# State space stage of a two-block transformer: transposes of x and y behind later products, half of the output additions on ScalarE and GpSimd

## The chip, the cores and the metric

The kernel runs on one core of a Trainium2 chip. The core has five engines with a queue of instructions each: TensorE (PE, matrix products and transposes), VectorE (DVE), ScalarE (ACT), GpSimd (POOL) and SyncE (SP, which issues DMAs). Each queue is worked off in order; semaphores make one engine wait for another. The metric is the time of one execution on the device in microseconds, the median over runs.

## The reference, cut to what matters

The program is two transformer blocks on 1024 tokens of width 1024, in float32. The change lies in the first layer of the second block. Its state space part and its convolution part share one input product and one output product:

```python
def even_layer(x, ...):
    proj = rmsnorm(x, norm_w) @ w_in
    z_a, xbc, dt_raw, glu_v, glu_g, z_b = jnp.split(proj, idx, axis=-1)
    xs, bs, cs = split(silu(causal_dwconv(xbc, conv_w, conv_b)))     # 4 taps
    y = ssd_chunked(xs, dt, a, bs, cs, d_skip) * silu(z_a)
    y_a = rmsnorm(y by group, ssd_norm_w)                            # 4 groups of 256
    u = causal_dwconv(glu_v * sigmoid(glu_g), dw_w, dw_b)            # 31 taps
    y_b = silu(layernorm(u, ln_w, ln_b)) * silu(z_b)
    return x + concatenate([y_a, y_b]) @ w_out

# ssd_chunked, for each chunk of 128 tokens and each head
y_diag = (cm @ bm.T * exp(segment sums)) @ (x * dt)
y_off  = exp(cs) * (cm @ state);   state = state * exp(cs[-1]) + bm.T @ (x * dt * decay)
y      = y_diag + y_off + x * d_skip
```

## The kernel before

Products of a weight with an activation are made from float32 numbers split in a high and a low part, three matmuls for one (L263 to L265, in `mm3`). ScalarE casts the high part of a weight (L197), VectorE and GpSimd subtract it from the weight for the low part (L202). PSUM gives four buffers of 512 columns (`pa`) and two of 1024 (`pb`), handed out in the order in which the program asks for them; a buffer is free for the next product when its last reader is done.

`even` makes the state space part in four groups g of four heads, and puts two of eight channel tiles of the convolution part into each group:

- z for eight token tiles (product, tanh on ScalarE, L1376 on VectorE), then a gated unit `glu`: two products in `pb`, a tanh, VectorE's L1331, and `conv31`, thirty VectorE steps (L1311) whose place in the queue is put back by 500 places, and which end in GpSimd's sum over channels, usum (L1312).
- `xbc` makes B, C and two tiles of x: product, three VectorE steps (L1351), a tanh on ScalarE (L1353) and a last step on VectorE (L1354). `x_tr(j, ...)` transposes a tile of x, tokens to partitions, in eight transposes on TensorE (L1408), with two copies on ScalarE (L1409).
- For each half i of the tokens (512): the product of B and C (L1453, copied by ScalarE at L1455), and for each of the four heads a segment product with its mask (L1459, L1460), the exponential on ScalarE (L1464) and the product with B C on GpSimd (L1465). This gives the matrices MT.
- For each half and each of its four token tiles m: y from MT x (L1484) and C state (L1485), VectorE (L1487, L1488), GpSimd (L1489, adds x d_skip) and VectorE (L1490, times silu z); and the new state (L1496, L1499).
- At the end of a half the four tiles of y are transposed back (L1505, eight transposes), scaled on ScalarE (L1508) and written to DRAM (L1509).
- Products of gate halves, z_b (`gate_half`: ScalarE L1341, VectorE L1342, which frees the PSUM buffer), are spread between these steps.

The order in which an engine takes its instructions is set by a planner that follows the order in which the code is written (its priority), put back or forward where `later` says so, and lets a ready instruction pass one that it expects to wait.

`conf` makes the output. `ya_load(g)` loads y of a group, casts it (ScalarE L1527) and subtracts (VectorE L1528); `out_proj` then makes for each of eight token tiles t and two halves hf of the columns six matmuls, and adds the result, times rstd, to h on VectorE (`add_h`, L292). Called y0 to y3 for the four groups. Between them stand the LayerNorm of the convolution part: the mean, u minus mu on VectorE (L1550), squares on ScalarE (L1555), their sum over eight channel tiles on GpSimd (L1556), and then u times rb (L1578, of each pair one on VectorE and one on GpSimd), which begins the four parts cp of the convolution part's output (L1580 to L1586, with additions at L290). In `out_proj` there is another way for half of the additions, `spread`, used by other stages of the kernel: ScalarE scales into a tile `tmp` (L305) and GpSimd adds it to h (L306).

## Time and profile before

| | us |
|---|---|
| median of three runs | 3098.76 (3096.89 to 3098.79) |
| the profiled execution | 3093.24 |
| its span, first to last instruction | 3091.2 |
| TensorE busy | 2907.2 |
| VectorE busy | 2062.9 |
| ScalarE busy | 1196.4 |
| GpSimd busy | 1014.5 |

The state space stage lies at about 1480 to 2190 us of the span, the output stage behind it until 2390. The rows below come from the page of the profile (busy times), from the view of who waited for whom, from the view of stretches of time with the granted clock of TensorE, from the groups by line, and from the timeline, in which an instruction's idle time before it stands in brackets with what ended it. Durations in the timeline are in us, those by line in ns.

### The profile page before, as it was taken

The numbers are of one execution on the slowest core, as the hardware profiler recorded it, in microseconds if no ns is written. First come the engines' busy times: TensorE is split into PE (matmuls) and PEld (weight loads), VectorE is DVE, ScalarE is ACT, GpSimd is POOL, SyncE is SP. The second block draws the span as 40 slices with busy tenths as digits, with TensorE's granted clock in tenths as the row PEclk, the third lists the DMA queues.
The fourth block names the chain that finished last, engine by engine and source line by source line (L and its number), as shares of the span: only waits on it lengthen the run. The fifth ranks groups of instructions, "written<-read, shape, count | busy, mean of one in ns | idle before, by whom it ended". The sixth has DMA issues, their size and how long they took to land.

```text
span 3091.2 us, 39184 instructions
## 1 busy us (share of the span) xinstructions
PE 2907.2 (94%) x14470; PEld 2364.7 (76%) x14470; DVE 2062.9 (67%) x3296; ACT 1196.4 (39%) x2264; POOL 1014.5 (33%) x917
## 2 busy tenths in 40 slices
PE   8999899898799999999998989999999999999998
PEld 7777676677588887788877878787777888878776
DVE  4225889865755555443798979787698454178786
ACT  5421666634433333221432322323234332155654
POOL 2112610122555554321125151524331231121444
PEclk9999999899899999999999999999999999999999
DMA  3012100212122223421311211122522446244531
GB/s 120 28 48 66 35 1 8 69 42 75 48 82 82 85 86 117 166 96 44 99 48 55 62 48 48 59 59 68 211 75 96 121 143 186 78 139 143 167 93 65
DMA packets 179380, 259.93 MB, mean 84 GB/s; under 512 B 16606, under 2 KB 107254, under 8 KB 179190
## 3 DMA queue, kind: packets, MB, share of 16 engines
q1 hardware_dynamic: 157813, 219.69, 22.4%
q10 hardware_dynamic: 16768, 20.98, 2.1%
q0 software_dynamic: 4608, 16.78, 1.4%
q8 instruction: 114, 1.87, 0.2%
q14 instruction: 77, 0.62, 0.1%
HBM read 191.33 MB, written 66.06 MB: 83 GB/s over the span
## 4 chain that ended last, share of the span: by engine, by line
PE 66%; DVE 15%; issue 5%; POOL 4%; ACT 3%; DMA 3%; SPq 0%; POOLq 0%; ACTq 0%; DVEq 0%
PE pa_t L263 16%; PE pa_t L264 16%; PE pa_t L265 15%; PE pb_t L265 3%; PE pb_t L264 3%; PE pb_t L263 3%; DVE acc_t L1311 3%; PE pa_t L941 2%; PE pb_t L1036 1%; PE pa_t L1055 1%; DVE wl_t L202 1%; PE pb_t L1750 1%; PE pb_t L1751 1%; ACT wh_t L197 1%; DVE h_t L292 1%
## 5 line engine op out<-in xcount | busy, mean ns | idle before, releaser
L202 POOL TENSOR_TENSOR wl_t<-wr_t,wh_t 128x349 fp32r<-128x349 f32 (+3 forms) x199 | 239.0, 1207 | 976.0 <-ACT wh_t L197 942.2
L263 PE MATMUL pa_t<-wh_t,x_t 128*128 128x512 f32 (+3 forms) x1024 | 374.3, 366 | 2.6 <-DVE xl_t L212 0.8
L264 PE MATMUL pa_t<-wl_t,x_t 128*128 128x512 f32 (+3 forms) x1024 | 371.3, 363 | 0.3 <-DVE wl_t L202 0.3
L1311 DVE SCALAR_TENSOR_TENSOR acc_t<-u_t,c,acc_t 128x1024 f32<-128x1024 f32 x240 | 339.4, 1416 | 2.9
L197 ACT CAST wh_t<-wr_t 128x1024 fp32r<-128x1024 f32 (+2 forms) x199 | 175.5, 890 | 354.2 <-PE pb_t L264 138.3
L290 DVE TENSOR_TENSOR h_t<-h_t,pa_t 128x512 f32<-128x512 f32 x256 | 173.1, 684 | 175.3 <-PE pa_t L265 171.8
L202 DVE TENSOR_TENSOR wl_t<-wr_t,wh_t 128x675 fp32r<-128x675 f32 (+2 forms) x173 | 170.9, 991 | 169.1 <-ACT wh_t L197 168.6
L263 PE MATMUL pb_t<-x_t,wh_t 128*128 128x512 f32 x608 | 244.3, 402 | 3.7 <-ACT wh_t L197 2.9
L265 PE MATMUL pb_t<-x_t,wl_t 128*128 128x512 f32 x608 | 242.2, 399 | 1.0 <-DVE wl_t L202 1.0
L264 PE MATMUL pb_t<-x_t,wh_t 128*128 128x512 f32 x576 | 231.0, 401 | 0.0
L265 PE MATMUL pa_t<-wh_t,x_t 128*128 128x512 f32 (+3 forms) x640 | 221.4, 346 | 0.0
L263 PEld LDWEIGHTS pa_t<-wh_t,x_t 128*128 128x128 f32 x1024 | 192.3, 188 | 33.6 <-ACT wh_t L197 1.8
L264 PEld LDWEIGHTS pa_t<-wl_t,x_t 128*128 128x128 f32 x1024 | 192.5, 188 | 30.9 <-DVE wl_t L202 2.0
L265 PE MATMUL pa_t<-wh_t,xl_t 128*128 128x512 f32 x512 | 200.4, 392 | 3.0 <-POOL xl_t L1848 2.1
L326 ACT CAST wh_t<-wr_t 128x512 fp32r<-128x512 f32 x154 | 92.1, 620 | 243.0 <-POOL wr_t L334 129.3
L263 PE MATMUL pa_t<-x_t,wh_t 128*128 128x512 f32 x400 | 163.9, 410 | 2.8 <-ACT xt_t L382 2.1
L265 PE MATMUL pa_t<-x_t,wl_t 128*128 128x512 f32 x400 | 158.8, 397 | 0.0
L327 DVE TENSOR_TENSOR wl_t<-wr_t,wh_t 128x512 fp32r<-128x512 f32 x110 | 97.7, 907 | 91.0 <-ACT wh_t L326 91.0
L263 PE MATMUL pa_t<-xh_t,wh_t 128*128 128x512 f32 x352 | 138.9, 395 | 5.3 <-DVE tmp_t L454 4.8
L263 PEld LDWEIGHTS pb_t<-x_t,wh_t 128*128 128x128 f32 x608 | 115.5, 190 | 30.8 <-ACT wh_t L197 3.9
L264 PE MATMUL pa_t<-xt_t,wh_t 128*128 128x512 f32 x352 | 138.2, 392 | 0.4 <-DVE xt_t L366 0.4
L265 PE MATMUL pa_t<-xh_t,wl_t 128*128 128x512 f32 x352 | 137.8, 392 | 0.0
(558 smaller groups left out, 7477.9 us busy)
## 6 DMA issues: line engine op xcount, KB each, us to landing
wr_t<-in_a_w_in SPq DMA_DIRECT2D x46, 512.0 KB
wr_t<-in_c_w_in SPq DMA_DIRECT2D x26, 512.0 KB
wr_t<-in_ffn_w_gate SPq DMA_DIRECT2D x22, 512.0 KB
wr_t<-in_ffn_w_up SPq DMA_DIRECT2D x22, 512.0 KB
yf<-o_t SPq DMA_DIRECT2D x22, 512.0 KB
wr_t<-in_ffn_w_down SPq DMA_DIRECT2D x44, 256.0 KB
yr_t<-yf SPq DMA_DIRECT2D x22, 512.0 KB
h_t<-in_x SPq DMA_DIRECT2D x16, 512.0 KB
```

The costliest lines, as they stand in the source:

```text
L197: nc.scalar.copy(hi, raw)
L202: e.tensor_tensor(*[x[:, c] for x in f], op=ALU.subtract)
L263: mm(out, lh, rh, start=st, stop=False)
L264: mm(out, lh, rl, start=False, stop=False)
L265: mm(out, ll, rh, start=False, stop=en)
L290: self.nc.vector.tensor_tensor(h[t][:, c], h[t][:, c], ps, op=ALU.add)
L292: self.nc.vector.scalar_tensor_tensor(h[t][:, c], ps, rstd[:, t:t + 1], h[t][:, c], op0=ALU.mult, op1=ALU.add)
L326: nc.scalar.copy(hi, src)
L327: eng.tensor_tensor(lo, src, hi.bitcast(F32), op=ALU.subtract)
L941: self.nc.tensor.transpose(pt[:, i * 256 + q * P:i * 256 + (q + 1) * P], w[t0 + q][:, (b0 + i) * P:(b0 + i + 1) * P], self.ident)
L1036: mm(sp[:, c0:c0 + wd], qT[:96, hd, t * P:(t + 1) * P], kT[:96, hd, c0:c0 + wd], start=True, stop=c0 + wd < n)
L1311: nc.vector.scalar_tensor_tensor(acc, u[:, k:k + S], cw31(k, c), acc, op0=ALU.mult, op1=ALU.add)
```

## The change

Three things. `x_tr(1, x1)`, the transposes of the group's second tile of x, moves from between the MT matrices of half 0 and those of half 1 to behind both. The transposes of y become a function `y_tr`, called later: for half 0 behind the first products (MT x and C state) of half 1, for half 1 behind the next group's first z product, and at once only at the very end. In `conf` the four y parts call `out_proj` with `spread=1`: in each token tile the second half's addition is made by ScalarE (L305) and GpSimd (L306), and the first half's stays on VectorE. The pool of `conf` gets two tmp tiles for it.

```diff
--- before.py
+++ after.py
@@ -1355,6 +1355,18 @@
             return o
 
         st8 = lambda tag: self.sb.tile([P, NT, 16], F32, name=tag, tag=tag, bufs=1)
+        turn_y = []
+
+
+        def y_tr(g, i, ys):
+            for j in range(2):
+                ps = self.psum()
+                for m in range(4):
+                    tr(ps[:, m * P:(m + 1) * P], ys[m][:, j * P:(j + 1) * P], self.ident)
+                yt = self.slot("zb", [P, 512])
+                nc.scalar.activation(yt, ps, AF.Copy, scale=gss[:, 2 * g + j:2 * g + j + 1])
+                nc.scalar.dma_start(out=ysp[2 * g + j, :, i * 512:i * 512 + 512], in_=yt)
+
         glu_w(0)
         for g in range(4):
             segs = [(g * 256, 256)] + ([(3072, 16)] if g == 0 else [])
@@ -1366,6 +1378,8 @@
             if g == 0:
                 dtr = st8("dtr")
             for t in range(NT):
+                if t == 1 and turn_y:
+                    y_tr(*turn_y.pop())
                 ps = self.psum()
                 nw = 272 if g == 0 else 256
                 tk = slice(t * P, (t + 1) * P)
@@ -1465,8 +1479,7 @@
                     nc.gpsimd.tensor_tensor(M, M, cb, op=ALU.mult)
                     MT[i, e] = M
                 spread()
-                if i == 0:
-                    x_tr(1, x1)
+            x_tr(1, x1)
             if g < 3:
                 glu(2 * g + 2)
             for i in range(2):
@@ -1483,6 +1496,8 @@
                     for e in range(4):
                         mm(ps[:, e * 64:(e + 1) * 64], MT[i, e][:, m * P:(m + 1) * P], xd[:, e * 64:(e + 1) * 64])
                     mm(ps[:, 256:512], cT[:, tk], state)
+                    if turn_y:
+                        y_tr(*turn_y.pop())
                     y = self.small(256, tag="y", bufs=4)
                     nc.vector.tensor_tensor(b4(y), b4(ps[:, 256:512]), self.bc(ecs[:, t, hs], 64), op=ALU.mult)
                     nc.vector.tensor_tensor(y, y, ps[:, 0:256], op=ALU.add)
@@ -1499,14 +1514,9 @@
                         nc.vector.tensor_tensor(ns, ns, ps[:, :256], op=ALU.add)
                         state = ns
                     spread()
-                for j in range(2):
-                    ps = self.psum()
-                    for m in range(4):
-                        tr(ps[:, m * P:(m + 1) * P], ys[m][:, j * P:(j + 1) * P], self.ident)
-                    c = slice(i * 512, i * 512 + 512)
-                    yt = self.slot("zb", [P, 512])
-                    nc.scalar.activation(yt, ps, AF.Copy, scale=gss[:, 2 * g + j:2 * g + j + 1])
-                    nc.scalar.dma_start(out=ysp[2 * g + j, :, c], in_=yt)
+                turn_y.append((g, i, ys))
+                if (g, i) == (3, 1):
+                    y_tr(*turn_y.pop())
             self.rsqrt(rstd, ss, 256 * 4, EPS, 8)
 
     def conf(self, hs, usum, rs, spill, zsp, ysp):
@@ -1527,7 +1537,7 @@
                 nc.scalar.copy(yh, y)
                 nc.vector.tensor_tensor(yl, y, yh.bitcast(F32), op=ALU.subtract)
                 ys.append((yh, yl))
-            return lambda ts=range(NT): self.out_proj(h, ys, w, rstd=rs[g], ts=ts)
+            return lambda ts=range(NT): self.out_proj(h, ys, w, rstd=rs[g], ts=ts, spread=1)
 
         y0 = ya_load(0)
         h = self.load_h(hs)
@@ -1994,7 +2004,7 @@
                     with K.pool("even", bc=2, u=2, sz=2, xs=2, bk=1, zb=2, MT=6, cb=1, tmp=2):
                         K.even(X, usum, rs, spill, zsp, ysp)
                 hctx = K.open(K.pool("h2", "right", h=8))
-                with K.pool("conf", u8=8, z=2, c=6, y2=8):
+                with K.pool("conf", u8=8, z=2, c=6, y2=8, tmp=2):
                     h, st = K.conf(hs, usum, rs, spill, zsp, ysp)
         if "E" in stages:
             h3 = dt("h3", [S, D])
```

Lines behind the change move: in `even` by 14 or 15 (L1408 becomes L1422, L1453 L1467, L1459 L1473), the transposes of y become L1365, and in `conf` lines move by 10 (L1556 becomes L1566, L1578 L1588).

TensorE, group 1, at the transposes of the second tile of x (`g_t`) before: `pb_t` products are those of the gated unit, `bc_t` those of B and C, `csT` the segment products.

```order
L263 MATMUL pb_t<-x_t,wh_t 128x512
L1408 MATMUL pa_t<-c_72,g_t 128x128 x8
L1453 MATMUL pa_t<-bc_t 128x128 x4
L1459 MATMUL pa_t<-csT,c_97 128x512
L1460 LDWEIGHTS c_99
L1460 MATMUL pa_t<-c_92,c_99 128x512
```

The same place after (the row here begins at the third of the segment products):

```order
L1473 MATMUL pa_t<-csT,c_97 128x512
L1474 LDWEIGHTS c_99
L1474 MATMUL pa_t<-c_92,c_99 128x512
L264 MATMUL pb_t<-x_t,wh_t 128x512
L1473 MATMUL pa_t<-csT,c_97 128x512
L1474 LDWEIGHTS c_99
L1474 MATMUL pa_t<-c_92,c_99 128x512
L1422 MATMUL pa_t<-c_72,g_t 128x128 x4
L265 MATMUL pb_t<-x_t,wl_t 128x512
L1422 MATMUL pa_t<-c_72,g_t 128x128 x4
L263 MATMUL pb_t<-x_t,wh_t 128x512
L264 MATMUL pb_t<-x_t,wh_t 128x512
```

The transposes of x stood first; they now stand behind the product of B and C, all four segment products and one product of the gated unit, and are cut in two.

TensorE, group 1, end of half 0, before: eight transposes of y stand ahead of half 1's first products (`xd_t,MT_t`, then `sst,bc_t`).

```order
L265 MATMUL pa_t<-x_t,wl_t 128x512
L1505 MATMUL pa_t<-c_72,y_t 128x128 x8
L1484 MATMUL pa_t<-xd_t,MT_t 128x64 x4
L1485 MATMUL pa_t<-sst,bc_t 128x256
L263 MATMUL pb_t<-x_t,wh_t 128x512
L1496 MATMUL pa_t<-xd_t,bk_t 128x256
L264 MATMUL pb_t<-x_t,wh_t 128x512
L265 MATMUL pb_t<-x_t,wl_t 128x512
L1484 MATMUL pa_t<-xd_t,MT_t 128x64 x4
```

After:

```order
L265 MATMUL pa_t<-x_t,wl_t 128x512
L1497 MATMUL pa_t<-xd_t,MT_t 128x64 x4
L1498 MATMUL pa_t<-sst,bc_t 128x256
L1365 MATMUL pa_t<-c_72,y_t 128x128 x8
L263 MATMUL pb_t<-x_t,wh_t 128x512
L264 MATMUL pb_t<-x_t,wh_t 128x512
L1511 MATMUL pa_t<-xd_t,bk_t 128x256
L265 MATMUL pb_t<-x_t,wl_t 128x512
L1497 MATMUL pa_t<-xd_t,MT_t 128x64 x4
```

The transposes of y have changed places with the first products of half 1; the next such product, which takes the second tile m, stands as far behind as before.

GpSimd, output stage, y0 to y2, before: usum additions L1556 (seven) between low parts of weights.

```order
L1489 TENSOR_TENSOR y_t<-y_t,xs_t 128x256
L202 TENSOR_TENSOR wl_t<-wr_t,wh_t 128x349
L1489 TENSOR_TENSOR y_t<-y_t,xs_t 128x256
L202 TENSOR_TENSOR wl_t<-wr_t,wh_t 128x349 x2
L1556 TENSOR_TENSOR usum_t<-usum_t,c_t 128x1024 x4
L202 TENSOR_TENSOR wl_t<-wr_t,wh_t 128x349
L1556 TENSOR_TENSOR usum_t<-usum_t,c_t 128x1024 x3
L202 TENSOR_TENSOR wl_t<-wr_t,wh_t 128x349 x3
```

After (L1566 is the usum addition, L306 the additions to h):

```order
L202 TENSOR_TENSOR wl_t<-wr_t,wh_t 128x349
L306 TENSOR_TENSOR h_t<-h_t,tmp_t 128x512 x4
L1566 TENSOR_TENSOR usum_t<-usum_t,c_t 128x1024 x2
L306 TENSOR_TENSOR h_t<-h_t,tmp_t 128x512
L1566 TENSOR_TENSOR usum_t<-usum_t,c_t 128x1024
L306 TENSOR_TENSOR h_t<-h_t,tmp_t 128x512
L1566 TENSOR_TENSOR usum_t<-usum_t,c_t 128x1024
L306 TENSOR_TENSOR h_t<-h_t,tmp_t 128x512
L1566 TENSOR_TENSOR usum_t<-usum_t,c_t 128x1024 x3
L306 TENSOR_TENSOR h_t<-h_t,tmp_t 128x512
L202 TENSOR_TENSOR wl_t<-wr_t,wh_t 128x349 x2
L306 TENSOR_TENSOR h_t<-h_t,tmp_t 128x512 x7
```

The seven usum additions now stand between the additions to h: two ahead of tile 4 of y1, the other five between tiles 4 and 7.

## Rows read from the trace of the kernel before

**Rows 1.** From the page, part 1: busy us (share of the span) xinstructions of each engine

```profile
PE 2907.2 (94%) x14470; PEld 2364.7 (76%) x14470; DVE 2062.9 (67%) x3296; ACT 1196.4 (39%) x2264; POOL 1014.5 (33%) x917
```

**Rows 2.** Busy time by engine in the output stage's first half (us, then busy (xinstructions) by engine)

```profile
2195.00:2300.00 105.00, 93.81 (x414) 73.96 (x412) 89.70 (x105) 33.97 (x34) 45.74 (x19) 1.00 0.41 152
```

**Rows 3.** Who TensorE waited for, 1480 to 2200 us: us in total, times, longest

```profile
PE pa_t L1408 <- DVE g_t L1354: 12.5, 5, 3.3
...
PE pa_t L1505 <- DVE y_t L1490: 7.4, 11, 1.3
```

**Rows 4.** The same for 2200 to 2330, 2230 to 2260 and 2285 to 2293 us

```profile
PE pa_t L263 <- DVE h_t L292: 8.8, 7, 1.6
...
PE pa_t L263 <- DVE h_t L292: 3.8, 3, 1.6
...
PE pa_t L263 <- DVE h_t L292: 2.0, 2, 1.2
```

**Rows 5.** Timeline of TensorE, group 1: start us, us, instruction [idle before <-releaser]

```profile
1785.63 1.06 PE L1408 MATMUL pa_t<-c,g_t 128*128 128x128 f32 x8 [3.09 <-DVE g_t L1354]
...
1791.13 0.39 PE L265 MATMUL pb_t<-x_t,wl_t 128*128 128x512 f32 x1
...
1791.36 0.40 PE L263 MATMUL pb_t<-x_t,wh_t 128*128 128x512 f32 x1
```

**Rows 6.** Timeline of VectorE and ScalarE, same place

```profile
1784.26 1.22 DVE L1354 SCALAR_TENSOR_TENSOR g_t<-g_t 128x1024 f32<-128x1024 f32 x1
...
1786.60 0.68 DVE L1342 SCALAR_TENSOR_TENSOR zb_t<-zb_t,pa_t 128x512 f32<-128x512 f32 x1
...
1784.13 0.58 ACT L1341 ACTIVATE zb_t<-pa_t 128x512 f32<-128x512 f32 x1
```

**Rows 7.** Windows behind the x waits of groups 0 and 1; PEclk after POOL is the granted clock

```profile
1624.50:1628.20 3.70, 3.42 (x24) 2.53 (x24) 3.70 (x6) 2.45 (x7) 1.67 (x2) 1.00 0.54 175
...
1785.50:1790.70 5.20, 5.07 (x24) 3.49 (x25) 5.17 (x6) 3.38 (x10) 1.77 (x3) 0.67 0.13 50
```

**Rows 8.** Timeline of VectorE at group 1's gated unit; GpSimd and TensorE in group 3

```profile
1811.87 1.22 DVE L1331 SCALAR_TENSOR_TENSOR u_t<-g_t,pb_t 128x1024 f32<-128x1024 f32 x1 [8.68 <-PE pb_t L265]
...
2130.83 2.36 POOL L1312 TENSOR_TENSOR usum_t<-usum_t,acc_t 128x1024 f32<-128x1024 f32 x1 [2.48 <-DVE acc_t L1311]
...
2133.24 1.98 PE L1543 MATMUL pb_t<-usum_t,c 128*128 128x512 f32 x4 [0.69 <-POOL usum_t L1312]
```

**Rows 9.** Timeline of TensorE and VectorE, end of half 0 and of half 1, group 1

```profile
1831.79 0.77 PE L1505 MATMUL pa_t<-c,y_t 128*128 128x128 f32 x5 [1.31 <-DVE y_t L1490]
...
1836.04 0.68 DVE L1342 SCALAR_TENSOR_TENSOR zb_t<-zb_t,pa_t 128x512 f32<-128x512 f32 x1
...
1836.77 1.10 PE L1484 MATMUL pa_t<-xd_t,MT_t 128*128 128x64 f32 x8 [1.22 <-DVE zb_t L1342]
...
1850.93 0.42 DVE L1490 TENSOR_TENSOR y_t<-y_t,sz_t 128x256 f32<-128x256 f32 x1 [0.64 <-POOL y_t L1489]
```

**Rows 10.** Instructions of three lines, whole kernel: xcount, ns min/median/max, first and last start, forms

```profile
L306 POOL TENSOR_TENSOR x_t<-x_t,tmp_t x49: 1259/1291/1951, 2886.2 to 3085.3; 128x512 f32<-128x512 f32 x49
...
L305 ACT ACTIVATE tmp_t<-pa_t,rsy_t x4: 687/688/689, 3072.6 to 3076.4; 128x512 f32<-128x512 f32 x4
...
L292 DVE SCALAR_TENSOR_TENSOR h_t<-pa_t,rsg_t,h_t x64: 733/741/752, 2193.2 to 2293.3; 128x512 f32<-128x512 f32 x64
```

**Rows 11.** The same for two usum additions and u times rb on GpSimd

```profile
L1556 POOL TENSOR_TENSOR usum_t<-usum_t,c_t x7: 2907/3282/3558, 2222.9 to 2249.7; 128x1024 f32<-128x1024 f32 x7
...
L1312 POOL TENSOR_TENSOR usum_t<-usum_t,acc_t x8: 2361/2406/3341, 1571.1 to 2130.8; 128x1024 f32<-128x1024 f32 x8
...
L1578 POOL TENSOR_TENSOR u_t<-u_t,c_t x4: 3389/3420/3462, 2276.0 to 2286.1; 128x1024 f32<-128x1024 f32 x4
```

**Rows 12.** Timeline of GpSimd and VectorE in the output stage

```profile
2237.98 3.43 POOL L1556 TENSOR_TENSOR usum_t<-usum_t,c_t 128x1024 f32<-128x1024 f32 x1 [4.84 <-ACT c_t L1555]
...
2240.38 4.00 DVE L1550 TENSOR_TENSOR u_t<-u_t,c_t 128x1024 f32<-128x1024 f32 x2
```

## The prediction

> **What bounds the kernel now.** The page comes first: TensorE is busy for 94% of the span [rows 1], and the waits that can be removed are short. In the output stage no other engine is full: of 105 us TensorE works 93.8, VectorE 89.7, ScalarE 34.0 and GpSimd 45.7 [rows 2]. So the change can take away only idle time of TensorE, and the view of who waited for whom gives its size. In the state space stage TensorE waits 12.5 us, five times, for the last step of the x convolution (L1354) before transposes of x, and 7.4 us, eleven times, for y (L1490) before transposes of y [rows 3]. In the output stage it waits 8.8 us, seven times, for additions into h (L292) [rows 4]. That is 28.7 us, 0.9% of the run. Then the timeline must tell, wait by wait, what is late next.
>
> **x behind the next products.** In group 1 TensorE ends the last product of a gate half and stands 3.09 us, until 1785.63, for L1354, which VectorE ends at 1785.48 [rows 5, 6]. The new order puts the product of B and C (four matmuls), three of the four segment products, one glu product and the fourth segment product ahead of the eight transposes. These have waits of their own. The third segment product needs a PSUM buffer that the copy of the B C product frees; that copy stands on ScalarE behind the tanh L1353 and the gate half's tanh, which ends at 1784.71 [rows 6], so with a copy of about the same 0.58 us it comes at 1785.3. The fourth needs the gate half's own buffer, freed by L1342, which VectorE runs behind L1354 and a convolution step and ends at 1787.28 [rows 6]. Hence waits of about 2.2 and 1.3 us where 3.09 us was. What is won is the work done in between. Fourth segment product, one glu product and transposes take about 1.7 us, until 1788.95, with 90 products of the gated unit left; before, the 90 began at 1790.7, two products ahead of the one at 1791.13; products follow each other every 0.23 us [rows 5]. Gain 1.7 us. The sum takes TensorE at full clock here. Before, the 5.2 us behind the wait had a granted clock of 0.67, a mix of 2.4 and 1.2 GHz; group 0, behind a shorter wait, kept 1.00 and did the same 24 matmuls in 3.7 us [rows 7]. If the two new waits bring the low clock too, the gain is about 1.1 us.
>
> Group 2 has the same waits: 1.7 again. In group 0 the third segment product waits for VectorE's gate half: 0.5. Does VectorE let these gains through? It idles 8.68 us for TensorE at the next gated unit, L1331 [rows 8], so it starts earlier by what TensorE gains (groups 0 and 2 have the same gap). In group 3 there is no later gated unit: the usum addition by GpSimd at 2130.83 ends VectorE's long convolution, and TensorE waits for it at 2133.24 [rows 8]. That chain moves with VectorE, by what groups 0 to 2 gave; the 3.3 us wait in front of x in group 3 is exchanged for this one. I count 0 for group 3, between -1 and +1. Sum for x: 0.5 + 1.7 + 1.7 = 3.9 us, less 0.2 for one worse y wait in group 2: **-3.7**, between -6 and 0.
>
> **y behind the next products.** Half 0: the 1.31 us wait at 1831.79 goes. But 5 us later TensorE stands 1.22 us at 1836.77 for a PSUM buffer that VectorE's L1342 frees at 1836.72 [rows 9]. VectorE reaches L1342 through L1490, whose input comes from GpSimd, and three convolution steps; the transposes feed none of these. TensorE arrives 1.3 us earlier and waits 1.3 us longer. Gain 0. Half 1: the last two transposes wait for the last y, which VectorE gives at 1851.35 [rows 9]; the planner has put as many z products ahead of them as before (36), so they wait together where three short ones of the eleven stood. Gain 0. Cost of the list itself: none, the same eight transposes, two copies and two DMAs a half, later. **0**, between -2 (half of the 7.4 us would need VectorE early) and +1. The edit moves waits and doesn't remove them.
>
> **Half of h's additions.** Removed from VectorE: 32 L292 of 0.74 us, 23.7 us. Added: 32 scaled copies on ScalarE and 32 additions on GpSimd. The same lines at the kernel's end show 0.69 us for the scaled copy, 1.29 us for the addition [rows 10]: 22 us and 41 us. ScalarE has room; GpSimd would have 46 + 41 = 87 of 105 us [rows 2], on average enough. But its queue is in order, and in y1 (see the order) seven usum additions stand between h's additions of tiles 3 and 7. With two tmp tiles and four PSUM buffers, the product of tile t and half 1 can't start before the addition of the tile four back and a 0.69 us copy.
>
> Before the addition of tile 7, GpSimd must do, from the addition of tile 3: seven usum additions and four h additions. One usum addition has a median of 3.28 us here and 2.41 us for the same shape elsewhere (L1312) [rows 11]; seven make 16.8 to 23.0 us, four additions 5.2: together 22 to 28. From the end of tile 3's product this begins after 0.69 + 1.29 = 2.0 us, and ends after 24 to 30 us; with the copy, 24.7 to 30.7. TensorE comes to tile 3 of y2 eight tiles later; twelve matmuls at 0.23 us a tile are 2.76 us, so after 8 x 2.76 - 1.38 = 20.7 us. **New stall: 4 to 10 us**, of which I take 7, the middle: the 3.28 us is a duration under contention, and VectorE keeps the instructions that contend (u minus mu, casts, weight remainders) and loses ones that don't. Against it: the waits there before, 3.8 us, go, and of the 3.0 us ahead of them (8.8 less 3.8 less 2.0 [rows 4]) 1.3 to 2.6, as y1's low half still waits for VectorE's cast behind h's load. Net 7 - 3.8 - 2 = 1.2, and about 0.8 for the additions that trail: **+2**, between -2.4 and +5.
>
> In y3 four products u times rb on GpSimd (3.42 us each [rows 11], 13.7 us) stand ahead of tile 3's addition. Stall 0.3 to 4.3 us, against 2.0 us of waits that go [rows 4]. What follows, the first conv part, starts when the chain of its second u (product, affine, tanh, two on VectorE, cast) is done; that chain is neither clearly shorter nor longer. **0**, between -3 and +3.
>
> How the exclusive use shows: GpSimd's usum addition at 2237.98 starts beside a VectorE u minus mu and takes 3.43 us; two u minus mu of 1.21 us each, started at 2240.38 while GpSimd is busy, take 4.00 us [rows 12]. The Trainium skill, page "SBUF — State Buffer", section "Who interferes with whom", has this as a rule: a VectorE instruction with two SBUF inputs and a GpSimd instruction that reads SBUF take one port pair in turn, for whole instructions, while VectorE with at most one SBUF input is free of it. The trace agrees (4.00 us against 2.4). By that rule L292, with one PSUM input, never held GpSimd up, and each of its replacements on GpSimd may hold VectorE up: it speaks against the edit. By the rule alone the sums would cost 3.28 us or more, and the time be that of rival B below; with sums as fast as L1312's it would be rival A's.
>
> **Sum:** -3.7 + 0 + 2 + 0 = -1.7 us. The profiled execution has 3093.24 us for a span of 3091.2; it would be 3091.5. The median of the runs shown is 3098.76, so the forecast is **3097 us**. About 0.2%, 6 us, is what a measurement of this kernel can tell from no change.
>
> **Rivals.**
> *A: GpSimd keeps up.* VectorE, with 23.7 us less, brings u minus mu forward, so the usum additions run in gaps before tile 3's addition, at 2.41 us. For it: GpSimd idles long ahead of the sums before, and 4 us, the low end of the stall, is by now as long as the 3.8 us that go. Against: the order nails five of the sums behind tile 4. Then no stall, -8.8 in the output stage and -3.7 before it: 3098.8 - 12.5 = **3086**. If the y waits went too (-28.7 in all): 3070, which needs VectorE to be early everywhere; inside this case, a tenth of it.
> *B, slower: GpSimd is the bound of the output stage.* 41 us of additions, 23 of sums, 13.7 of products and what VectorE locks (up to 27 us, 22 instructions of 1.2 us) make 105 us against 105 us. ScalarE then stands at its scaled copy for a tmp tile, and casts and squares behind it come late, which delays the sums again. Stall 10 in y1 and y2, 4 in y3, against 5.8 + 2 us that go, and 3 us for the conv chain, x keeping only 1: 10 + 4 + 3 - 7.8 - 1 = +8: **3107**. It decides when the sums cost 3.28 us or more in the new order.
> *C: the edits do only what the order says and each wait is replaced* (x's too, by the low clock or by VectorE): -1 to +2, **3099**; inside the forecast's case.
>
> **How the numbers follow.** Forecast and C together 0.49, A 0.30, B 0.21. The forecast's bounds are -6 - 2.4 - 3 = -11.4 and 0 + 5 + 3 = +8, or 3087 to 3107; A's and B's middles lie at the ends, so the range is 3085 to 3108. Faster by over 0.2%: 0.30; within: 0.49; slower: 0.21.
>
> **What would show it.** In the profile after: no 3 us waits at the x transposes but two shorter ones, at the third and fourth segment products, and a granted clock near 1.00 there; y's waits of TensorE falling while the waits for L1342 grow by as much; in the output stage a wait of several us in y2 for tmp tiles or ScalarE, with usum additions of 2.4 to 3.3 us just ahead; VectorE some 24 us less busy and GpSimd 41 us more. I am wrong if y's waits go without replacement, or if TensorE has no wait above 2 us in y2.

## The result, and the profile after

The changed kernel takes 3115.16 us (median of 5 runs, 3114.07 to 3123.33) and the kernel before, beside it, 3098.76 us (5 runs, 3096.89 to 3107.0). The ratio is 1.0056 with an interval from 1.0039 to 1.0073: slower by 17.4 us, between 12 and 23 (the two medians lie 16.4 apart). The forecast was 3097 us with a range up to 3108. So the time lies outside it, and on the side of rival B.

The profiled execution after has 3118.79 us; the one before had 3093.24. Between these two lie 25.5 us, 8 more than the ratio gives, so some of what the two traces differ by belongs to the executions and not to the change. The page's engine line, to be held against [rows 1]:

```profile
PE 2928.4 (94%) x14466; PEld 2381.3 (76%) x14470; DVE 2058.4 (66%) x3264; ACT 1216.1 (39%) x2296; POOL 1055.2 (34%) x949
```

VectorE loses 32 instructions; ScalarE and GpSimd gain 32 each, as the diff says. GpSimd's busy time grows by 40.7 us (41 were forecast) and ScalarE's by 19.7. VectorE's falls by only 4.5 where 23.7 us of additions left it. TensorE has the same products and is busy for 21.2 us longer, which a lower granted clock does: 0.971 over the run where 0.980 was.

Two windows for each kernel show where the time went: the state space stage (from the first gated unit, L1331, to the last L1342 of a gate half) and the output stage up to the last addition L292. Columns as in [rows 2]: length, busy time of TensorE, of its weight loads, of VectorE, ScalarE and GpSimd, granted clock, DMA share, GB/s. Before:

```profile
1514.10:2186.20 672.10, 634.04 (x3283) 523.99 (x3282) 575.31 (x625) 199.27 (x387) 250.23 (x228) 0.99 0.19 57
...
2186.20:2293.30 107.10, 96.13 (x426) 75.89 (x424) 88.23 (x119) 35.43 (x37) 47.32 (x21) 1.00 0.44 165
```

After:

```profile
1515.50:2193.10 677.60, 643.50 (x3279) 532.88 (x3282) 573.65 (x625) 199.10 (x387) 240.73 (x228) 0.97 0.19 56
...
2193.10:2313.80 120.70, 101.61 (x427) 78.71 (x425) 85.39 (x89) 53.49 (x67) 91.61 (x50) 0.94 0.40 146
```

The state space stage is 5.5 us longer. Its idle time fell by about 4 us (38.1 to 34.1, length less busy), but TensorE is busy for 9.5 us more at a clock of 0.97. The output stage is 13.6 us longer: idle time of TensorE rises by 8.1 us (11.0 to 19.1), busy time by 5.5. The other 6.6 of the 25.7 us between the spans lie outside both windows: 1.5 right behind the second, the rest where nothing was changed.

Who TensorE waited for, 1480 to 2200 us after (us in total, times, longest), against [rows 3]:

```profile
PE pa_t L1473 <- DVE zb_t L1342: 7.8, 4, 3.4
PE pa_t L1511 <- DVE zb_t L1342: 6.2, 4, 2.6
PE pa_t L1497 <- DVE zb_t L1342: 3.5, 2, 2.0
PE pa_t L1473 <- ACT cb_t L1469: 3.1, 2, 1.6
PE pa_t L1511 <- ACT zb_t L1367: 2.7, 2, 1.4
PE pa_t L1365 <- DVE y_t L1505: 2.4, 5, 0.6
```

Of the 12.5 us in front of the transposes of x 0.8 are left, and of the 7.4 in front of those of y (now L1365) 2.4. In their places stand waits for L1342 and for two copies on ScalarE (L1469 of B C, L1367 of the transposed y), at the segment products (L1473), the products of MT and x (L1497) and the state update (L1511). The same view for the output stage, 2200 to 2400 us, against [rows 4]:

```profile
PE pa_t L263 <- ACT tmp_t L305: 9.7, 2, 6.9
PE pa_t L263 <- DVE h_t L292: 6.5, 6, 1.8
```

The waits for VectorE's L292 did not go with half of its instructions: 6.5 us where 8.8 were. Two waits for the scaled copy L305 are new, one of them a stall of 6.9 us.

### The profile page after: what moved, and what is told of

Same layout as the page of the kernel before. It is cut to its first block, busy times and chain, and to the rows that moved or that the text cites. A ratio compares the mean times of both kernels' runs of the same rounds, so it can differ in the third digit from the quotient of the medians.

```text
span 3116.9 us, 39226 instructions
## 1 busy us (share of the span) xinstructions
PE 2928.4 (94%) x14466; PEld 2381.3 (76%) x14470; DVE 2058.4 (66%) x3264; ACT 1216.1 (39%) x2296; POOL 1055.2 (34%) x949
## 4 chain that ended last, share of the span: by engine, by line
PE 66%; DVE 13%; POOL 5%; issue 5%; ACT 4%; DMA 3%; SPq 0%; POOLq 0%; ACTq 0%; DVEq 0%
PE pa_t L263 16%; PE pa_t L264 15%; PE pa_t L265 15%; PE pb_t L265 3%; PE pb_t L263 3%; PE pb_t L264 3%; DVE acc_t L1311 3%; PE pa_t L941 2%; PE pb_t L1036 1%; PE pb_t L1760 1%; PE pa_t L1055 1%; DVE wl_t L202 1%; PE pb_t L1761 1%; ACT wh_t L197 1%; POOL wl_t L202 1%
## 5 line engine op out<-in xcount | busy, mean ns | idle before, releaser
L290 DVE TENSOR_TENSOR h_t<-h_t,pa_t 128x512 f32<-128x512 f32 x256 | 172.9, 683 | 174.5 <-PE pa_t L265 171.0
L265 PEld LDWEIGHTS pb_t<-x_t,wl_t 128*128 128x128 f32 x608 | 116.1, 191 | 28.8 <-DVE wl_t L202 2.7
```

The lines of the kernel that those rows point to most:

```text
L265: mm(out, ll, rh, start=False, stop=en)
L290: self.nc.vector.tensor_tensor(h[t][:, c], h[t][:, c], ps, op=ALU.add)
```

## The experiments

All twelve were timed against the kernel before. "us" is the ratio less one, times 3098. The last two columns are read from the one profiled execution of each run: the lengths in us of the state space stage (first L1331 to last L1342) and of the output stage (from there to its last L290). They are 672.1 and 196.9 before and 677.5 and 211.9 after.

| run | what it is | ratio (interval) | us (interval) | state space | output |
|---|---|---|---|---|---|
| e1_x | x moved alone | 0.9999 (0.9991 to 1.0008) | -0.3 (-2.8 to +2.5) | 670.9 | 196.7 |
| e2_y | y moved alone | 1.0013 (1.0004 to 1.0022) | +4.0 (+1.2 to +6.8) | 675.5 | 196.8 |
| e3_spread | half of h's additions alone | 1.0048 (1.0036 to 1.0060) | +14.9 (+11 to +19) | 670.9 | 213.3 |
| e5_tmp4 | e3_spread, four tmp tiles | 1.0038 (1.0023 to 1.0052) | +11.8 (+7 to +16) | 673.3 | 206.2 |
| e6_sumv | e3_spread, usum additions on VectorE | 1.0030 (1.0018 to 1.0042) | +9.3 (+6 to +13) | 672.9 | 204.0 |
| e7_allv | e6_sumv, products u times rb there too | 1.0004 (0.9995 to 1.0014) | +1.2 (-1.5 to +4.3) | 671.2 | 195.8 |
| e11_spread_fill | e3_spread, stall filled with products | 1.0050 (1.0031 to 1.0069) | +15.5 (+10 to +21) | 673.1 | 210.1 |
| e4_warm | before, x wait filled with products | 0.9995 (0.9986 to 1.0003) | -1.5 (-4.3 to +0.9) | 673.2 | 195.8 |
| e8_yfill | e2_y, wait filled with products | 1.0017 (1.0004 to 1.0030) | +5.3 (+1.2 to +9.3) | 680.3 | 195.9 |
| e9_y_half0 | only half 0's transposes of y moved | 1.0005 (0.9991 to 1.0018) | +1.5 (-2.8 to +5.6) | 675.5 | 196.4 |
| e10_y_half1 | only half 1's | 1.0006 (0.9995 to 1.0018) | +1.9 (-2.8 to +5.6) | 672.4 | 197.6 |
| e12_allv_warm | e7_allv and e4_warm together | 0.9996 (0.9986 to 1.0006) | -1.2 (-4.3 to +1.9) | 673.4 | 196.7 |

The stage lengths vary less than whole executions do. The output stage, where no edit touches it, lasts 195.8 to 197.6 us in seven executions; the state space stage, where the transposes of y of half 0 stay in place, 670.9 to 673.4 us in ten. They are each from one execution, though, and have no interval.

**The three edits apart.** Each is its own part of the diff, put into the kernel before (of the part for y the fence shows the calls in the loop over halves alone). The theory after reading the trace was that the state space stage lost by the clock and the output stage by GpSimd; the rival was the forecast's own terms.

```diff
-                if i == 0:
-                    x_tr(1, x1)
+            x_tr(1, x1)
```

> Only the transposes of the second x tile moved. Theory (waits and clock): the waits of TensorE fall by 3 to 4 us as forecast, but behind the new pair of waits the granted clock falls (0.53 to 0.59 for 3 to 4 us in groups 0 and 1 of the whole change), so the time changes by -2 to +2 us. Rival (waits alone count): -3.7 us, as the prediction's sum had it.

Measured -0.3 us: no gain, and -3.7 lies outside the interval. The theory's range holds, but not its reason: behind the two waits in group 1 the clock was 1.00 here.

```diff
...
+                    if turn_y:
+                        y_tr(*turn_y.pop())
...
+                turn_y.append((g, i, ys))
+                if (g, i) == (3, 1):
+                    y_tr(*turn_y.pop())
```

> Only the transposes of y moved. Theory (waits and clock): behind the first products of half 1 two or three waits now follow each other with little work between, TensorE's granted clock falls to 0.5 to 0.6 for about 6 us in groups 0 to 2; +5 to +8 us over the kernel before. Rival (the waits only change places, as the prediction said): 0, between -2 and +1.

Measured +4.0 us, slower as the theory had it, but less than the +5 to +8 it asked.

```diff
-            return lambda ts=range(NT): self.out_proj(h, ys, w, rstd=rs[g], ts=ts)
+            return lambda ts=range(NT): self.out_proj(h, ys, w, rstd=rs[g], ts=ts, spread=1)
...
-                with K.pool("conf", u8=8, z=2, c=6, y2=8):
+                with K.pool("conf", u8=8, z=2, c=6, y2=8, tmp=2):
```

> Only half of the additions into h by ScalarE and GpSimd. Theory (GpSimd's queue with its exclusive use against VectorE, then the clock): +12 to +15 us, all between 2190 and 2330 us of the span, a stall of 6 to 8 us at tile 3 of y2 and a granted clock of about 0.8 behind it. Rival (the whole loss is the output stage's): +16 to +17. Prediction's sum: +2.

Measured +14.9 us, at the upper end of the theory's range. The three make 18.6 us together, 17.4 were measured: the parts add up, and the spread additions are most of it.

**What in the output stage costs 14.9 us.** In the changed kernel's y2 the row of the stall on TensorE, then GpSimd's queue ahead of it (start us, us, instruction [idle before <-releaser]):

```profile
2264.31 0.80 PE L263 MATMUL pa_t<-wh_t,y_t 128*128 128x512 f32 x1 [6.90 <-ACT tmp_t L305]
```

```profile
2250.83 1.91 POOL L306 TENSOR_TENSOR h_t<-h_t,tmp_t 128x512 f32<-128x512 f32 x1
2252.70 9.62 POOL L1566 TENSOR_TENSOR usum_t<-usum_t,c_t 128x1024 f32<-128x1024 f32 x3
2262.28 1.25 POOL L306 TENSOR_TENSOR h_t<-h_t,tmp_t 128x512 f32<-128x512 f32 x1
```

GpSimd has no idle time from 2231.8 to 2270. Three usum additions of 3.2 us stand ahead of the addition that frees a tmp tile; it ends at 2263.5, the scaled copy follows at 2263.57, TensorE at 2264.31. Three runs ask whether it is the number of tiles or GpSimd's queue.

```diff
-                with K.pool("conf", u8=8, z=2, c=6, y2=8, tmp=2):
+                with K.pool("conf", u8=8, z=2, c=6, y2=8, tmp=4):
```

> Half of the additions into h moved (as in e3, nothing else of the change), with four tmp tiles instead of two. Theory (GpSimd's late additions hold ScalarE's scaled copies, and so PSUM, through the tmp tiles): two more tiles let TensorE run on for up to two token tiles, 5.5 us; the 6 to 7 us stall falls to 0 to 2 us, the clock stays up, and of e3's loss of 15 us some 9 to 12 go: +3 to +6 against before. Rival (VectorE, held up by GpSimd's instructions, is what sets the end): the waits move to L292 and to the casts of y, +10 to +15.

Measured +11.8 us, where the theory asked +3 to +6 and the rival +10 to +15. The trace gives the tiles more weight than the time does: every engine works in the order of e3_spread, the stall of 6.9 us is gone, and the output stage lasts 206.2 us instead of 213.3. So two tmp tiles make part of the loss, and four don't end it. GpSimd runs the same queue, and the wait is for L292 instead (waits of TensorE, 2190 to 2400 us, then GpSimd):

```profile
PE pa_t L263 <- DVE h_t L292: 11.8, 8, 2.6
```

```profile
2249.30 9.69 POOL L1556 TENSOR_TENSOR usum_t<-usum_t,c_t 128x1024 f32<-128x1024 f32 x3
2258.95 1.30 POOL L306 TENSOR_TENSOR h_t<-h_t,tmp_t 128x512 f32<-128x512 f32 x1
```

Next the other work of GpSimd goes back to VectorE, first the seven usum additions, then the four products as well:

```diff
-                nc.gpsimd.tensor_tensor(sqs, sqs, sq, op=ALU.add)
+                nc.vector.tensor_tensor(sqs, sqs, sq, op=ALU.add)
```

> As e3, but the seven usum additions of the output stage are on VectorE instead of GpSimd (8.5 us more for VectorE, 23 us less for GpSimd). Theory: no stall in y1 and y2, what is left is y3, where four products on GpSimd stand ahead of h's additions: 0 to +4 us against before. Rival (VectorE is the bound): as e3 or worse, +12 to +18.

```diff
-                (nc.gpsimd if j else nc.vector).tensor_tensor(u, u, rb, op=ALU.mult)
+                nc.vector.tensor_tensor(u, u, rb, op=ALU.mult)
```

> As e6, and the four products u times rb that GpSimd had are on VectorE too: GpSimd does h's additions and low parts of weights alone. Theory: -5 to +1 us against before, as the 8.8 us of waits for L292 go and little comes for them. Rival (VectorE is the bound): the conv chain grows by 4 x 1.2 us and waits for y_t rise: +3 to +6.

Measured +9.3 and +1.2 us; the first lies between what theory and rival asked. Without the sums the stall in y2 is gone and one in y3, behind the four products, is left; without the products that one is gone too. Waits of TensorE for tmp tiles, 2190 to 2400 us, in e6_sumv (e7_allv has no such row):

```profile
PE pa_t L263 <- ACT tmp_t L305: 2.9, 1, 2.9
```

So nearly all of the 14.9 us hangs on the two kinds of work sharing GpSimd's queue with the additions. The split is rough: 5.6 us on the sums and 8.1 on the products by the middle values of the times, whose intervals touch, 9.3 and 8.2 us by the output stage (213.3, 204.0, 195.8). What is left, +1.2, is no gain either. Whether the sums and products cost by standing in the queue or by what GpSimd and VectorE slow in each other, these runs can't tell, as both leave with them. VectorE's groups in e7_allv (count | busy us, mean ns):

```profile
L1550 DVE TENSOR_TENSOR u_t<-u_t,c_t 128x1024 f32<-128x1024 f32 x8 | 14.5, 1828 | 0.0
...
L1556 DVE TENSOR_TENSOR usum_t<-usum_t,c_t 128x1024 f32<-128x1024 f32 x7 | 11.2, 1600 | 0.0
```

A usum addition takes 1.6 us on VectorE and 3.28 on GpSimd [rows 11]. The additions into h still take 1.58 us each on GpSimd in e7_allv and u minus mu 1.83 on VectorE, so what these two slow in each other is still there, and without the stalls it costs nothing that shows.

The last run of this group asks whether the low clock behind the stall (0.90 for the 25 us from 2257.2 in e3_spread) is part of the price. It fills the stall with 24 products whose result is overwritten, and moves no other instruction:

```diff
...
+                if fill and t == 3 and hf == 0:
+                    for _ in range(24):
+                        self.nc.tensor.matmul(ps, lhs[0][0], rhs[0][0])
...
```

> As e3, with 24 products (5.5 us, result overwritten) ahead of the first half of tile 3 of y2, where TensorE stands for 6.9 us; no other instruction has another place. Theory (part of e3's loss is the lower clock behind that stall): granted clock 1.00 from there on to 2285, 2.5 to 4 us less than e3: +10 to +12 us against before. Rival (GpSimd's queue sets the pace there whatever TensorE's clock): as e3, +13 to +16.

Measured +15.5 us, no different from e3_spread. The stall is filled but for 0.68 us, and the clock behind it is full (TensorE's timeline, then the window; lines stand three further down in this kernel):

```profile
2257.09 5.76 PE L304 MATMUL pa_t<-wh_t,y_t 128*128 128x512 f32 x24
...
2264.93 0.50 PE L263 MATMUL pa_t<-wh_t,y_t 128*128 128x512 f32 x1 [0.68 <-ACT tmp_t L308]
```

```profile
2264.90:2289.90 25.00, 24.96 (x124) 20.84 (x125) 10.66 (x21) 8.26 (x12) 17.81 (x15) 1.00 0.26 85
```

The wait still ends when GpSimd's queue lets it. Behind it TensorE is faster: from the last L1342 to the last L292 the trace has 118.9 us at a granted clock of 0.99, where e3_spread has 120.9 and the changed kernel 120.7, both at 0.94. So some 2 us of the loss may be the clock's. The times can't tell that from nothing, and they don't show the theory's 2.5 to 4.

**Why x gains nothing.** The forecast read its gain of 1.7 us against [rows 5], an execution in which the clock fell to 0.67 behind the 3.09 us wait [rows 7]. In e3_spread the order of the state space stage is that of before, the wait is 3.10 us in groups 1 and 2, and behind it the windows are:

```profile
1784.30:1789.50 5.20, 3.51 (x24) 2.62 (x25) 5.20 (x7) 3.31 (x9) 1.28 (x2) 1.00 0.14 52
1944.90:1950.10 5.20, 4.97 (x24) 4.08 (x25) 5.07 (x7) 2.67 (x8) 1.53 (x2) 0.69 0.14 54
```

The first is at full clock, the second not: the same wait and order, either level. And the stretch in question in group 1, from the start of the fourth L1331 (1725.99 before) to that of the fifth (1811.87), has these lengths, as differences in us to the 85.88 of before:

| | before | after | e1_x | e3_spread | e7_allv | e11_spread_fill | e6_sumv | e10_y_half1 | e5_tmp4 | e4_warm |
|---|---|---|---|---|---|---|---|---|---|---|
| order of x | old | new | new | old | old | old | old | old | old | old, filled |
| granted clock | 0.98 | 0.98 | 1.00 | 1.00 | 1.00 | 1.00 | 0.98 | 0.98 | 0.96 | 1.00 |
| us | 0 | -0.20 | -1.68 | -1.62 | -1.63 | -1.63 | +0.03 | +0.06 | +1.35 | -0.89 |

At 1.00 the old order shows the "gain" of e1_x to 0.06 us, and at 0.98 the new order is 0.2 to 0.3 us ahead of the old. It was the clock of the one profile that I had. In group 2 (sixth to seventh L1331) it is the same: at 1.00 the stretch is 1.67 us shorter than before in the changed kernel and 1.56 in e2_y, with the old order of x; at 0.98 it is 0.24 us shorter in e1_x and 0.18 in e3_spread. The run that gives the full clock without the move has ten products with an overwritten result ahead of the transposes of x:

```diff
+                    if j == 1 and i == 0:
+                        for _ in range(10):
+                            mm(ps, xh[0][:, 0:P], xh[0][:, 0:512])
```

> The kernel before, with ten products of 512 columns, whose result is overwritten, ahead of the transposes of the second x tile, so that TensorE works where it waited (2.3 us in group 0, 3.1 to 3.3 in groups 1 to 3). No step is taken away and no dependency changed. Theory (clock): granted clock 1.00 in the 5 us behind the place instead of 0.67 (groups 1, 2) and 0.51 (group 3); 1.5 us less in each of groups 1 and 2 and up to 3 in group 3: -3 to -6 us. Rival (the lower clock there costs nothing, since VectorE sets the pace): 0 to +1.

Measured -1.5 us, not told from nothing, and between what theory and rival asked. In group 1 the stretch is 0.89 us shorter, 0.7 less than in the old order at full clock without products. The clock behind the wait was 1.00, and yet TensorE still waited for VectorE's L1354 at the transposes of x (here L1411):

```profile
1786.16 1.09 PE L1411 MATMUL pa_t<-c,g_t 128*128 128x128 f32 x8 [1.41 <-DVE g_t L1354]
```

```profile
1786.10:1791.30 5.20, 5.14 (x29) 3.94 (x31) 5.20 (x7) 3.74 (x11) 2.23 (x3) 1.00 0.14 54
```

**Why y costs some 4 us.** The runs with one half each are e2_y with another condition for the transposes at once:

```diff
                 turn_y.append((g, i, ys))
-                if (g, i) == (3, 1):
+                if i:
+                    y_tr(*turn_y.pop())
```

> Of the move of y's transposes only half 0 (behind the first products of half 1). Theory (the cost of e2 sits here: GpSimd's xdd and x d_skip come ahead of VectorE's convolution steps, L1342 is 0.95 us later, and two waits stand behind each other): +3 to +5 us against before. Rival (the cost sits in half 1, whose transposes now wait together in the next group): 0 to +1.

```diff
                 turn_y.append((g, i, ys))
-                if (g, i) == (3, 1):
+                if not i or g == 3:
+                    y_tr(*turn_y.pop())
```

> Of the move of y's transposes only half 1 (behind the next group's first z product). Theory (cost in half 0): -1 to +1 us against before. Rival (cost in half 1): +3 to +4.

The times, +1.5 and +1.9 us, tell neither half from nothing nor from the other. The traces do better: the state space stage lasts 675.5 us with half 0 moved (e2_y, e9_y_half0) and 672.4 with half 1 alone, where 670.9 to 673.4 were seen without half 0. So half 0 costs some 3 us and half 1 nothing. The stretches between the starts of the third and the fourth, the fifth and the sixth, and the seventh and the eighth L1331 hold the ends of half 0 in groups 0, 1 and 2. They are longer than before by 1.56, 2.25 and 0.78 us in e9_y_half0, by 0.12, 0 and -0.13 in e10_y_half1, and by 1.93, 1.10 and 1.58 after. VectorE shows why. The end of half 0 in group 0, first before, then after, in each the last product of y, three steps of the convolution and the L1342 that frees a PSUM buffer:

```profile
1670.55 0.42 DVE L1490 TENSOR_TENSOR y_t<-y_t,sz_t 128x256 f32<-128x256 f32 x1 [1.19 <-POOL y_t L1489]
1670.89 4.46 DVE L1311 SCALAR_TENSOR_TENSOR acc_t<-u_t,c,acc_t 128x1024 f32<-128x1024 f32 x3
1675.28 0.67 DVE L1342 SCALAR_TENSOR_TENSOR zb_t<-zb_t,pa_t 128x512 f32<-128x512 f32 x1
```

```profile
1673.44 0.82 DVE L1505 TENSOR_TENSOR y_t<-y_t,sz_t 128x256 f32<-128x256 f32 x1 [1.19 <-POOL y_t L1504]
1674.19 5.02 DVE L1311 SCALAR_TENSOR_TENSOR acc_t<-u_t,c,acc_t 128x1024 f32<-128x1024 f32 x3
1679.12 0.68 DVE L1342 SCALAR_TENSOR_TENSOR zb_t<-zb_t,pa_t 128x512 f32<-128x512 f32 x1
```

From the product of y to L1342 it was 4.73 us and is 5.68: 0.95 us later. Both longer rows are instructions with two SBUF inputs. GpSimd at that time, after:

```profile
1673.38 0.60 POOL L1493 TENSOR_TENSOR xd_t<-xs_t,dtds 128x256 f32<-128x256 f32 x1
1674.06 0.68 POOL L1494 TENSOR_TENSOR xs_t<-xs_t,c 128x256 f32<-128x256 f32 x1
```

Before, GpSimd had nothing between 1670.5 and 1672.6 (it waited for a weight), and these two came only at 1674.24, behind the weight's part. With the y transposes out of the way, half 1's products are issued earlier in the program, and these two with them, into VectorE's last product and first convolution step. e9_y_half0 shows the same 5.68 us (1671.13 to 1676.81), e10_y_half1 the 4.73 of before (1670.07 to 1674.80). In group 1 the delay after is 0.95 us again, in group 2, with two convolution steps there, 0.6: 2.5 us in all. TensorE's three waits at this place in group 0 are 0.39, 1.37 and 1.99 us where 1.32, 0.28 and 1.21 were: 0.94 us more. The middle one is for ScalarE's copy of the transposed y (L1367), which now has less work between it and the product that needs its buffer; the forecast had not counted it. The window behind them is at a low clock after, and also in e10_y_half1 (first and second fence):

```profile
1679.80:1684.00 4.20, 4.14 (x15) 3.69 (x15) 3.02 (x7) 0.00 (x0) 2.63 (x4) 0.50 0.45 147
```

```profile
1675.50:1679.70 4.20, 4.18 (x18) 3.72 (x18) 3.01 (x6) 0.41 (x1) 3.58 (x5) 0.59 0.44 143
```

e10_y_half1 had the low clock too, with the order of before, in which the first profile had 1.00, and its group 0 was only 0.12 us longer. So in the old order the clock costs next to nothing in this place, and the late L1342, which comes with half 0 alone, is left as a cost. With half 0 moved, though, the stretch is the longer the lower its clock is: in group 0 +0.97 us in e2_y (granted clock over the stretch 0.98), +1.56 in e9_y_half0 and +1.93 after (both 0.96); in group 2 +0.78 in e2_y and e9_y_half0 (0.98) and +1.58 after (0.94). Group 1 doesn't bear on it: +1.10 to +2.25 us, all at 0.96. No run has this order at full clock there, so the clock's share is not shown. The run that was to settle it put 14 products of 128x256 into the wait of groups 0 to 2:

```diff
+                        if i and not m and g < 3:
+                            for _ in range(14):
+                                mm(ps[:, 256:512], xh[0][:, 0:P], xh[0][:, 0:256])
```

> Transposes of y moved as in e2, with fourteen products of 256 columns (result not used) behind the first state product of half 1 in groups 0 to 2, where TensorE waits 2 us for VectorE's L1342; no dependency changed. Theory (the clock is what the move costs): no clock below 0.9 in the 6 us behind, e2's +4 us becomes 0, between -2 and +2. Rival (the later L1342 itself is the cost): +4 to +6 as e2.

It is inconclusive. The clock was not held: in the 6 us behind the fill it was 0.96, 0.80 and 0.90 in groups 0, 1 and 2, and in group 2 it was low in the fill itself (below, group 1 behind the fill, then group 2 in it).

```profile
1844.20:1850.20 6.00, 3.92 (x18) 3.20 (x19) 5.29 (x10) 0.86 (x3) 4.02 (x4) 0.80 0.55 163
...
2010.80:2015.00 4.20, 4.20 (x24) 4.15 (x23) 3.59 (x7) 0.77 (x2) 1.63 (x1) 0.60 0.33 125
```

And +5.3 us is not e2_y's order alone, as the fill also put VectorE's state update behind another instruction of its queue, with a new wait of TensorE:

```profile
1685.90 0.70 PE L1499 MATMUL pa_t<-sst,bc_t 128*128 128x256 f32 x2 [1.55 <-DVE sst L1518]
```

**Both pieces that looked best.** e7_allv with the fill of e4_warm, 13 products in groups 1 to 3:

```diff
+                        for _ in range(13 if g else 10):
+                            mm(ps, xh[0][:, 0:P], xh[0][:, 0:512])
```

> e7 (half of h's additions on ScalarE and GpSimd, sums and products of the output stage on VectorE) and e4 (products whose result is overwritten in the wait ahead of the second x tile, thirteen in groups 1 to 3) together. Theory (waits for L292 shortened, clock kept): -2 to -6 us against before. Rival (both gains are below what can be measured): -1 to +2.

Measured -1.2 us (-4.3 to +1.9): no version tried here is told from the kernel before on the fast side.

## Why the prediction was wrong

Right were the reading that TensorE bounds the kernel and only short waits were to be had, and most places of the new waits; the size of the new stall came out by luck. Wrong was what these do to the time, by 18 us.

**x, -3.7 us forecast, -0.3 measured.** The order did what was forecast: two waits in group 1 where 3.09 us was. The third and the fourth segment product:

```profile
1790.07 0.50 PE L1473 MATMUL pa_t<-csT,c 128*128 128x512 f32 x1 [1.56 <-ACT cb_t L1469]
...
1792.16 0.79 PE L1473 MATMUL pa_t<-csT,c 128*128 128x512 f32 x1 [1.14 <-DVE zb_t L1342]
```

They are 1.56 and 1.14 us, 2.2 and 1.3 were forecast. The step that failed is "The sum takes TensorE at full clock here", set against a row of before that was at 0.67. e1_x had the full clock in group 1 and shows the forecast gain, 1.68 us, and three runs with the old order at full clock show it too. Behind the second wait the clock is 0.53 in the changed kernel (in group 0, which stood at 1.00 in [rows 7], it is 0.59 behind a wait of 2.19):

```profile
1627.80:1632.00 4.20, 4.12 (x15) 2.81 (x16) 4.13 (x4) 0.59 (x1) 3.31 (x3) 0.59 0.16 62
1792.10:1795.50 3.40, 3.34 (x12) 2.65 (x13) 3.37 (x3) 0.59 (x1) 3.28 (x3) 0.53 0.20 77
```

One side of the subtraction had a clock that the other was not given. At equal clock the two orders reach the next gated unit within 0.3 us of each other. The idle time of the stage fell by 4 us in the profile after, and it is the wrong thing to count: there it was exchanged for busy time at a lower clock.

**y, 0 forecast, +4.0 measured.** The steps on TensorE hold in part: the 1.31 us wait fell to 0.4 and the waits for L1342 grew, but a wait of 1.37 us for the copy of y came too. The step that failed is "the transposes feed none of these". They feed nothing on VectorE's way to L1342, but they stood in the program ahead of half 1's instructions, and two of those, on GpSimd, now run earlier and beside VectorE's. The forecast asked what the transposes feed and not what comes forward on the other engines when they leave. Its bounds for y were -2 to +1, with no term on the slow side for it, and the sum of bounds then left them out; with them it would be 3085 to 3108, the range as stated. Half 1, forecast at 0, is 0 in the traces.

**Half of h's additions, +2 forecast, +14.9 measured.** The stall, taken at 7 us, is 6.90, but that is luck. Both ends of the subtraction came some 5.6 us late. The scaled copy of tile 3 of y1 starts at

```profile
2231.00 0.69 ACT L305 ACTIVATE tmp_t<-pa_t,rsg_t 128x512 f32<-128x512 f32 x1 [2.06 <-PE pa_t L265]
```

and from there GpSimd and the last copy need 33.3 us, until 2264.3, where 24.7 to 30.7 were forecast: seven sums at the upper end (23.1 us) and four additions at 7.7 us, not 5.2. TensorE came after 26.4 us (2264.31 less 6.90), not 20.7: it had waited 3.1 us for L292 on the way, at a granted clock of 0.94. The rest of the term failed in three steps. "The 3.8 us go, and of the 3.0 us ahead of them 1.3 to 2.6", 5.8 us in all, were credited for VectorE's lighter load. In the trace 2.1 us went (6.8 before, in y0 to y2; 4.7 after, with a new wait of 1.6 us for VectorE's low part of y, L1538). Groups of VectorE and GpSimd, 2190 to 2400 us (count | busy us, mean ns | idle before); L1560 was L1550. First before:

```profile
L292 DVE SCALAR_TENSOR_TENSOR h_t<-pa_t,rsg_t,h_t 128x512 f32<-128x512 f32 x64 | 45.4, 742 | 10.7 <-DMA h_t<-hs 7.1 <-PE pa_t L265 3.5
...
L1550 DVE TENSOR_TENSOR u_t<-u_t,c_t 128x1024 f32<-128x1024 f32 x8 | 12.2, 1534 | 0.0
```

After:

```profile
L306 POOL TENSOR_TENSOR h_t<-h_t,tmp_t 128x512 f32<-128x512 f32 x32 | 50.1, 1572 | 25.2 <-ACT tmp_t L305 19.8 <-DMA h_t<-hs 5.3
L1566 POOL TENSOR_TENSOR usum_t<-usum_t,c_t 128x1024 f32<-128x1024 f32 x7 | 22.9, 3266 | 0.2
```

```profile
L292 DVE SCALAR_TENSOR_TENSOR h_t<-pa_t,rsg_t,h_t 128x512 f32<-128x512 f32 x32 | 23.5, 744 | 27.1 <-PE pa_t L265 19.1 <-DMA h_t<-hs 8.0
L1560 DVE TENSOR_TENSOR u_t<-u_t,c_t 128x1024 f32<-128x1024 f32 x8 | 17.0, 2158 | 0.0
```

VectorE lost 21.9 us of L292 and got back part of it in the instructions that stayed: u minus mu took 1.53 us on average and takes 2.16. GpSimd's additions into h take 1.57 us on average, not 1.29. The forecast quoted the exclusive use and its rows [rows 12] and then charged it to the sums alone; what it does to VectorE's own instructions was left to rival B. The Trainium skill, page "SBUF — State Buffer", section "Who interferes with whom", puts it both ways: a VectorE instruction with two SBUF inputs and a GpSimd instruction that reads SBUF contend for one pair of ports under an exclusive lock, and which of them waits is a matter of which was issued first. The trace agrees, with 2.16 us against 1.53 on VectorE and 1.57 against 1.29 on GpSimd.

The second step is y3 and conv, forecast at 0. There the waits rose by 3.6 us (4.7 to 8.4), and the stretch behind the last L292 by 1.5. e6_sumv and e7_allv put about 8 us on the four products u times rb, which the forecast had at a stall of 0.3 to 4.3 us less 2.0. The third is the clock, for which the term had nothing: TensorE is busy for 5.5 us more in the output stage, at 0.94 where 1.00 was, and e11_spread_fill puts some 2 us of the loss on it.

**Rivals.** B was the mechanism: GpSimd sets the pace of the output stage where the sums cost 3.28 us; e7_allv shows it, as the loss goes when GpSimd's other work does. Its price was +8 for a sum with x at -1; the edit costs 15, as B credited 7.8 us of waits that mostly stayed. A would have needed the sums in gaps; [rows 12] and the order spoke against it, and it did not happen. C fits x alone. B's chance of 0.21 was too low, and 3107 too low as its end: the range would have had to carry the waits that stay, y3 and the clock. The two signs by which the forecast would be wrong, y's waits going without replacement and no wait above 2 us in y2, both looked for a faster kernel; neither came, and VectorE's busy time, which was to fall by 24 us, fell by 4.5.

**What stays open.** How much of half 0's cost is the late L1342 and how much the clock: 2.5 us is the sum of the delays of L1342, some 3 us what the stage became longer. How the cost of the sums and products divides between GpSimd's order and what it and VectorE slow in each other. And why one execution's clock falls behind a 3.1 us wait and another's doesn't; the runs show only that both happen with one order.

## What to carry to other kernels

Before work is moved to an engine because its average load leaves room, write down its queue in order at the place where the consumer waits, and charge every instruction that both engines slow in each other to both. When an instruction is moved out of the way, ask what comes forward on every engine that was issued behind it. And do not take a gain from a row at a lowered clock: look for the same place in another group or execution at the other level first.

## What was not expected of the hardware

The granted clock behind one and the same wait differs between executions and groups: 1.00 and 0.69 behind 3.10 us in e3_spread, 1.00 and 0.59 (before, e10_y_half1) behind 1.21 us. Behind a wait filled with products it was 1.00 in e4_warm and e11_spread_fill, but 0.80 in group 1 of e8_yfill. No fill made a measured time shorter by more than 2.4 us (e12_allv_warm against e7_allv), which is within the uncertainty; in e11_spread_fill's trace the output stage up to the last L292 is 2 us shorter than in e3_spread.
